# A GLU output stage in five passes over its tokens, with four token tiles' third quarter at the end

## The chip, the cores and the metric

The kernel runs on one core of a Trainium2 chip. The metric is the device time of one execution in microseconds (us), as a median over several executions; lower is better. The engines are named as in the profile: PE (matrix multiplies and transposes), DVE (vector operations), ACT (activations, copies and casts), POOL, and SP, which issues nearly all DMAs. Each engine runs its own instructions strictly in the order in which they were placed in its stream and waits for others by semaphores.

## The reference, cut to what matters

The model is a decoder trunk of two layers that runs on a prompt of 1024 tokens and on 64 sample tokens. Layer 0 mixes with a state-space model whose output goes through a gated linear unit (GLU), is normed, is added to the residual, and then goes through a convolutional feed-forward net (FFN):

```python
z = jax.nn.gelu(y).astype(u.dtype)
gl = z @ w_glu                                     # w_glu: 1024 x 2048
out = gl[..., :D_MODEL] * jax.nn.sigmoid(gl[..., D_MODEL:])
...
x = x + rmsnorm(a_out, p['a_post_g'][i])           # x1: goes to DRAM and on
f_out, buf = conv_ffn(rmsnorm(x, p['f_pre_g'][i]), ...)   # first step: h = x @ w_up
```

`rmsnorm(x, g)` is `x * rsqrt(mean(x*x) + eps) * g` over the 1024 channels of a token.

## The kernel before, in words

**Tiles.** Tokens lie in eight prompt tiles of 128 (numbers 0 to 7) and one sample tile of 64 (`NTT`, number 8). Multiplies are done in float32 split into a high and a low part, so each product is three matmuls (`mm3`, L800 to L802); the parts of the input are `xT_hi` and `xT_lo`, those of a weight `whi` and `wlo`.

**The GLU stage** (`glu`) runs four passes, one for each quarter `q` of the output channels (256 of them, with their 256 gates). In a pass, `tok_mm` does 24 matmuls of 128x512 for each prompt tile (16 for the sample tile) in the order `ORDER_U = [0, 3, 1, 4, 2, 5, 6, NTT, 7]`; then ACT takes the sigmoid of the gate half (L1022) and DVE multiplies (L1023) into columns `q*256...` of `ao[tt]`, an `acc` slot of 1024 columns that is held for the tile from the first pass to the last. A pass needs four units of weights (`load_w`): two DMAs of 256 KB into one of two `raw` buffers, a cast to `whi` on ACT (L783) and a subtraction to `wlo` on DVE (L784). `whi` and `wlo` rotate through 11 slots.

**The tails.** In the last pass, `tail.add` follows each tile's product. `tail_a` loads the residual row `xr` (L825), takes the sum of squares over 1024 columns on ACT (L815), multiplies by the post-norm gain over 1024 columns on DVE (L829), forms the reciprocal root in eight small DVE operations (`rstd_from`, L118 to L126), multiplies and adds the residual (L832) and stores the row to `x1d` (L833). `tail_n` does square, root and gain of the next norm (L842). Two tiles later (`lag`) `pop` transposes the tile on PE (L848) and splits it into `xT_hi` (ACT, L136) and `xT_lo` (DVE, L137). For the pairs of tiles (0,3), (1,4), (2,5), `Combos.pair` first forms four sums and differences of the two (L889 to L892, DVE), and transposes these, for the fast multiplication that follows.

**The FFN's first step** (`ffn_up(0)`) loads two blocks of `w_up`, forms their sums on DVE (L1076 to L1079, in the two `xr` slots) and begins with product p1 over tiles 0 to 2, first on channels 0 to 511 and then on the others; the next products need the combinations of all three pairs; the last ones need tiles 6, 7 and `NTT`.

**Order.** A scheduler sets the order of instructions on each engine when the kernel is built; tile pools (`acc` 14 slots, `gr` 5, `xr` 2) tell when a buffer is free again.

Of the kernel before, what the change touches and what calls it, by code (L numbers as in the profile page):

```python
# [20 lines left out]
P = 128  # L21
# [52 lines left out]
def trunk_kernel(ctx, tc, I, O):  # L74
# [33 lines left out]
    def flat(t, n=512):  # L108
        return t[:, 0:n]

    def rstd_from(pool, ss, n, parts, tag, n_mean=D, bufs=None):

        kw = {"bufs": bufs} if bufs else {}
        v = pool.tile([P, n], F32, tag=tag + "v", name=nm("rv"), **kw)
        s = pool.tile([P, n], F32, tag=tag + "s", name=nm("rs"), **kw)
        r = pool.tile([P, n], F32, tag=tag + "r", name=nm("rr"), **kw)
        p = slice(0, parts)
        V.tensor_scalar(v[p], ss, -0.5 / n_mean, -0.5 * EPS, op0=ALU.mult, op1=ALU.add)  # L118
        V.tensor_scalar(r[p].bitcast(I32), v[p].bitcast(I32), -0.5, RSQ_MAGIC, op0=ALU.mult, op1=ALU.add)
# [684 lines left out]
    def tokens(tt):  # L804
        return (tt * P, P) if tt < NTT else (SEQ, TS)
# [6 lines left out]
    def square_sum(y, n):  # L812
        junk = slot("junk", dtype=BF16)
        ss = slot("ss")
        A.activation(junk[0:n], y, AF.Square, accum_out=ss[0:n])  # L815
        return ss[0:n]

    def rms_rstd(t, n):
        return rstd_from(pools["ph"], square_sum(t, n), 1, n, "n1", bufs=4)

    def tail_a(y, tt, post, xsrc, xdst, last=False):

        t0, n = tokens(tt)
# [74 lines left out]
    class Tail:  # L898
# [6 lines left out]
        def add(self, y, tt, *a):  # L905
            tail_a(y, tt, *a)
# [86 lines left out]
    def glu(ws):  # L993

        zt = slot("acc")[0:TS, 0:D]
        zv = zt.rearrange("r (b g c) -> r b g c", g=8, c=16)
        for u in range(3):
            for j in range(min(3, 8 - 3 * u)):
                zs = zsd.rearrange("(b u) r w -> u r b w", u=3)[u, 32 * j : 32 * j + NB]
                nc.sync.dma_start(zv[:, :, 3 * u + j], zs.rearrange("s b (t c) -> (s t) b c", c=16))  # L1000
        post = row_bcast(I["a_post_g"][0])
        tail.gain = row_bcast(I["f_pre_g"][0])
        ao = {}
        for q in range(4):
            if q:
                ws = glu_units(q)
            qs_ = slice(q * 256, (q + 1) * 256)
            for tt in ORDER_U:
                n = tokens(tt)[1]
                if q == 0:  # L1010
                    ao[tt] = slot("acc")
                    if tt == ORDER_U[4]:
                        tail_b(zt, NTT)
                        xsx = sample_pair()
# [6 lines left out]
                sg = slot("gr")  # L1021
                A.activation(sg[0:n, 0:256], g[:, 256:512], AF.Sigmoid)  # L1022
                V.tensor_tensor(ao[tt][0:n, qs_], g[:, 0:256], sg[0:n, 0:256], ALU.mult)  # L1023
                if q == 3:
# [1006 lines left out]
```

## Time and profile before

| | |
|---|---|
| median of 3 executions | 2728.16 us (2722.85 to 2728.78) |
| the profiled execution, its own time | 2735.15 us |
| its span in the trace | 2733.4 us |
| PE busy | 2508.6 us, 92% of the span |
| DVE busy | 1958.1 us, 72% |
| ACT busy | 1261.3 us, 46% |
| POOL busy | 688.7 us, 25% |
| mean granted clock of PE | 0.972 |

The profile is one execution; the time of 2735.15 us is that execution's, and the 1.75 us beyond its span lie around it. A share of busy time is a mean over stages that differ, so the rows further below are taken from the stretch in which the GLU stage ends and the FFN begins (225 to 520 us). In a row, "idle before <- releaser" tells how long an engine stood still before an instruction and what ended that. PEclk 1.00 is the upper level of the matrix engine's clock, 2.4 GHz; values between 0.5 and 1.00 are means over a stretch with both levels.

### The profile page before, as it was taken

The page shows a single profiled execution, that of the slowest core. Times are in us where ns is not written, and L with a number is a line of the kernel's source. Part 1 is how long each engine was busy: PE and PEld are TensorE (multiplying, and loading weights), DVE is VectorE, ACT ScalarE, POOL GpSimd, SP SyncE. Part 2 cuts the span into 40 slices and gives each one's busy share as a digit, 9 for nine tenths or more (in the row PEclk, how much of TensorE's full clock was granted, in tenths as well). Part 3 has the DMA queues.
Part 4 walks back from the last instruction along what each step waited for, and adds up shares of the span by engine and source line. Part 5 has one row for each costly group of instructions (what it writes and reads, how often), then busy time and mean ns, then how long its engine had stood idle before and what let it go on. Part 6 is the DMA issues. An engine that isn't in the chain of part 4 may idle for free. (4 is left out here: it accounts for less than half of the span.)

```text
span 2733.4 us, 39285 instructions
## 1 busy us (share of the span) xinstructions
PE 2508.6 (92%) x14234; PEld 2203.3 (81%) x14234; DVE 1958.1 (72%) x3721; ACT 1261.3 (46%) x2477; POOL 688.7 (25%) x943
## 2 busy tenths in 40 slices
PE   3878997999999989999999899999699999998995
PEld 3767886999999967778776788877599999996774
DVE  7993349677777699884223688966877767779998
ACT  6762224444444454344322677853544444454332
POOL 3220000111332275401211222200011222237651
PEclk9999998999999999999999999999899999999998
DMA  5432322122222233344646433325222222233324
GB/s 143 106 93 76 92 65 92 61 73 74 77 79 75 91 110 90 113 138 174 204 154 206 107 87 83 92 85 171 85 73 72 73 72 73 72 108 102 103 82 146
DMA packets 257701, 278.61 MB, mean 102 GB/s; under 512 B 41772, under 2 KB 205924, under 8 KB 257508
## 3 DMA queue, kind: packets, MB, share of 16 engines
q1 hardware_dynamic: 253188, 263.85, 31.3%
q0 software_dynamic: 3232, 10.29, 1.7%
q8 instruction: 113, 1.85, 0.3%
q10 hardware_dynamic: 1088, 1.97, 0.2%
q14 instruction: 80, 0.66, 0.1%
HBM read 187.82 MB, written 68.58 MB: 94 GB/s over the span
## 5 line engine op out<-in xcount | busy, mean ns | idle before, releaser
L800 PE MATMUL mm<-xT_hi,whi 128*128 128x320 f32 (+1 forms) x1408 | 459.4, 328 | 6.1 <-ACT xT_hi L136 2.8
L801 PE MATMUL mm<-xT_lo,whi 128*128 128x320 f32 (+1 forms) x1408 | 456.3, 324 | 0.1
L802 PE MATMUL mm<-xT_hi,wlo 128*128 128x384 f32 (+1 forms) x1408 | 454.7, 324 | 0.0
L1162 POOL COPY cvo<-acc 128x2 f32<-128x2 f32 x88 | 157.4, 1788 | 675.6 <-ACT acc L1145 675.6
L137 DVE TENSOR_TENSOR wlo<-raw,whi 128x1024 fp32r<-128x1024 f32 x88 | 107.6, 1222 | 239.4 <-PE mm L801 233.3
L800 PEld LDWEIGHTS mm<-xT_hi,whi 128*128 128x128 f32 x1408 | 265.1, 189 | 15.1 <-DVE acc L1128 9.6
L801 PEld LDWEIGHTS mm<-xT_lo,whi 128*128 128x128 f32 x1408 | 266.1, 189 | 0.9 <-DVE xT_lo L137 0.9
L802 PEld LDWEIGHTS mm<-xT_hi,wlo 128*128 128x128 f32 x1408 | 265.5, 189 | 0.3
L1159 DVE SCALAR_TENSOR_TENSOR acc<-acc,cpar,acc 128x1104 f32<-128x1104 f32 x176 | 239.3, 1380 | 0.8 <-ACT acc L1157 0.5
L800 PE MATMUL mm<-whi,xT_hi 128*128 128x512 f32 x576 | 228.5, 401 | 4.0 <-ACT whi L783 4.0
L801 PE MATMUL mm<-wlo,xT_hi 128*128 128x512 f32 x576 | 229.1, 399 | 0.5 <-DVE wlo L784 0.5
L802 PE MATMUL mm<-whi,xT_lo 128*128 128x512 f32 x576 | 229.1, 399 | 0.0
L136 ACT CAST whi<-raw 128x1024 fp32r<-128x1024 f32 x88 | 92.6, 1052 | 282.3 <-PE mm L802 265.7
L1384 DVE TENSOR_TENSOR acc<-mm,acc 128x512 f32<-128x512 f32 x279 | 184.3, 680 | 11.1 <-PE mm L802 10.2
L800 PE MATMUL mm<-acc,whi 128*128 128x384 f32 x528 | 179.6, 341 | 4.9 <-DVE acc L1119 3.1
L801 PE MATMUL mm<-acc,whi 128*128 128x384 f32 x528 | 179.5, 340 | 0.0
L802 PE MATMUL mm<-acc,wlo 128*128 128x384 f32 x528 | 179.4, 340 | 0.0
L800 PEld LDWEIGHTS mm<-whi,xT_hi 128*128 128x128 f32 x576 | 108.7, 189 | 33.2 <-ACT whi L783 4.2
L801 PEld LDWEIGHTS mm<-wlo,xT_hi 128*128 128x128 f32 x576 | 108.8, 189 | 26.8 <-DVE wlo L784 0.9
L802 PEld LDWEIGHTS mm<-whi,xT_lo 128*128 128x128 f32 x576 | 108.8, 189 | 26.6 <-issue 0.8
L1157 ACT ACTIVATE acc<-acc,cpar 128x1104 f32<-128x1104 f32 x88 | 115.4, 1313 | 30.9 <-DVE acc L1128 20.2
L1846 DVE CUSTOM_DVE_ANT_0 S<-mm,tb 128x512 f32<-128x512 f32 (+3 forms) x192 | 101.2, 552 | 29.0 <-PE mm L1844 25.7
(561 smaller groups left out, 6238.6 us busy)
## 6 DMA issues: line engine op xcount, KB each, us to landing
raw<-in_w_up_dram SPq DMA_DIRECT2D x88, 512.0 KB
gd<-acc SPq DMA_DIRECT2D x44, 552.0 KB
raw<-in_w_down_dram SPq DMA_DIRECT2D x44, 512.0 KB
gr<-gd SPq DMA_DIRECT2D x80, 256.0 KB
raw<-in_glu_w_dram SPq DMA_DIRECT2D x32, 256.0 KB
acc<-in_cache_k_dram SPq DMA_DIRECT2D x16, 512.0 KB
acc<-in_cache_v_dram SPq DMA_DIRECT2D x16, 512.0 KB
xj<-in_x_prompt_dram SPq DMA_DIRECT2D x8, 512.0 KB
```

Of the source, the lines that this page charges most:

```text
L136: A.copy(hi_ap, ps_ap)
L137: V.tensor_tensor(lo_ap, ps_ap, hi_ap.bitcast(F32), ALU.subtract)
L800: PE.matmul(out, lh, rh, start=start, stop=False, **kw)
L801: PE.matmul(out, lh, rl, start=False, stop=False, **kw)
L802: PE.matmul(out, ll, rh, start=False, stop=stop, **kw)
L1157: A.activation(hc, hb[:, 2 : 2 + TG], AF.Identity, bias=cp[:, ft, 3:4], scale=cp[:, ft, 2:3])
L1159: V.scalar_tensor_tensor(hc, hb[:, tap : tap + TG], cp[:, ft, tap : tap + 1], hc, op0=ALU.mult, op1=ALU.add)
L1162: GP.tensor_copy(co[:, 0:2], hb[:, SEQ : SEQ + 2])
L1384: V.tensor_tensor(a, ps, a, ALU.add)
L1846: V.tensor_tensor_reduce(S_[j][:, k0 : k0 + w], ps[:, 0:w], H["tb"][:, b0 : b0 + w], 0.125, -3e38, ALU.add, ALU.max, mx[:, j, c : c + 1])
```

## The change

Five passes take the place of four, as (quarter, tiles, tiles whose tail follows):

- quarter 0, all tiles; quarter 1, all tiles;
- quarter 2, only `EARLY = [NTT, 0, 3, 1, 4]`;
- quarter 3, all tiles in the order `ORDER_O = [NTT, 0, 3, 1, 4, 2, 5, 6, 7]`; the tails of `EARLY` follow their products here;
- quarter 2 again, only `LATE = [2, 5, 6, 7]`, with their tails.

The weights of quarter 2 are therefore loaded, cast and subtracted twice. For a tile's quarters other than its last, the new `part` takes the sum of squares over 256 columns (ACT), adds it to a running sum (`pre`, DVE, L834) and multiplies by the post-norm gain (DVE, L838). `tail_a` then squares and multiplies only the last 256 columns, and `rstd_from` takes the running sum in. The four late tiles no longer hold an `acc` slot from the first pass on: their quarters 0, 1 and 3 are formed in the free half of a `gr` slot, stored to a DRAM tensor `aod` (12 stores of 128 KB), and come back in the last pass (8 loads, 512 and 256 columns) into an `acc` slot taken there. No matmul and no transpose is added or taken away.

```diff
+    EARLY, LATE = ORDER_O[:5], ORDER_O[5:]
...
+    def part(y, tt, post, cs):
+
+        n = tokens(tt)[1]
+        ss = square_sum(y, n)
+        if tt in sums:
+            p = sums[tt]
+            V.scalar_tensor_tensor(p, ss, -0.5 / D, p, op0=ALU.mult, op1=ALU.add)
+        else:
+            p = sums[tt] = pools["ph"].tile([P, 1], F32, tag=f"pre{tt}", name=nm("pre"), bufs=1)[0:n]
+            V.tensor_scalar(p, ss, -0.5 / D, -0.5 * EPS, op0=ALU.mult, op1=ALU.add)
+        V.tensor_tensor(y, y, post[0:n, cs], ALU.mult)
...
-        ss = square_sum(y, n)
-        for hs in halves:
+        ss = square_sum(y[:, rest], n)
+        for hs in halves if last else (rest,):
             V.tensor_tensor(y[:, hs], y[:, hs], post[0:n, hs], ALU.mult)
-        r = rstd_from(pools["ph"], ss, 1, n, "n1", bufs=4)
+        r = rstd_from(pools["ph"], ss, 1, n, "n1", bufs=4, pre=sums.pop(tt, None))
...
-        for q in range(4):
-            if q:
+        for q, tts, end in ((0, ORDER_U, ()), (1, ORDER_U, ()), (2, EARLY, ()), (3, ORDER_O, EARLY), (2, LATE, LATE)):
+            if q or end:
                 ws = glu_units(q)
...
+                if end is LATE:
+                    for cs in (slice(0, 512), slice(768, D)):
+                        nc.sync.dma_start(ao[tt][:, cs], aod[t0 : t0 + n, cs])
...
+                yq = ao[tt][0:n, qs_] if tt in ao else sg[:, 256:512]
+                V.tensor_tensor(yq, g[:, 0:256], sg[:, 0:256], ALU.mult)
+                if tt in end:
...
+                    tail.add(ao[tt][0:n, 0:D], tt, post, x_in, x_scr(x1d), rest=qs_)
+                else:
+                    part(yq, tt, post, qs_)
+                    if tt in LATE:
+                        nc.sync.dma_start(aod[t0 : t0 + n, qs_], yq)
+                        tail.norm()
+                        tail.pop()
```

In the changed kernel's order the lines have moved: L805 to L807 are the matmuls (before L800 to L802), L868 the transposes (L848), L141 the low-part evacuations (L137), L1049 the GLU product (L1023), L849, L852 and L862 the post-norm product, the residual and the gain (L829, L832, L842), L909 to L912 the pair's sums (L889 to L892), L783 the loads of GLU weights (L778), L1107 to L1110 the sums of `w_up` (L1076 to L1079).

**PE where the GLU stage ends.** Before, behind the last three GLU matmuls (`mm_3945`, the last prompt tile) stand eight groups of four transposes (the rest of tile 1, the five of the pair (1,4), two of tile 2; `gr` is a pair's sum or difference, `acc` a tile's normed row), and then the FFN's first product `mm_4103`:

```order
L800 MATMUL mm_3945<-whi_3314,xT_hi 128x512
L801 MATMUL mm_3945<-wlo_3315,xT_hi 128x512
L802 MATMUL mm_3945<-whi_3314,xT_lo 128x512
L848 MATMUL tr_3755<-ident,acc_2401 128x128 x4
L848 MATMUL tr_3832<-ident,gr_3824 128x128 x4
L848 MATMUL tr_3839<-ident,acc_2430 128x128 x4
L848 MATMUL tr_3846<-ident,gr_3825 128x128 x4
L848 MATMUL tr_3855<-ident,gr_3826 128x128 x4
L848 MATMUL tr_3864<-ident,gr_3827 128x128 x4
L848 MATMUL tr_3931<-ident,acc_2459 128x128 x4
L848 MATMUL tr_3938<-ident,acc_2459 128x128 x4
L800 MATMUL mm_4103<-xT_hi,whi_4081 128x384
```

Of the changed kernel, behind the last GLU matmuls (`mm_4138`, tile 7) stand two groups, of tile 2, and then the FFN's first product `mm_4261`:

```order
L806 MATMUL mm_4138<-wlo_3950,xT_hi 128x512
L807 MATMUL mm_4138<-whi_3949,xT_lo 128x512
L868 MATMUL tr_4200<-ident,acc_3955 128x128 x4
L868 MATMUL tr_4207<-ident,acc_3955 128x128 x4
L805 MATMUL mm_4261<-xT_hi,whi_4239 128x384
L806 MATMUL mm_4261<-xT_lo,whi_4239 128x384
L807 MATMUL mm_4261<-xT_hi,wlo_4240 128x384
L805 MATMUL mm_4261<-xT_hi,whi_4239 128x384
```

After the first 12 matmuls of that product come the transposes of the pair (2,5); `gr_4290` is that pair's first difference and `acc_4005` tile 5:

```order
L805 MATMUL mm_4261<-xT_hi,whi_4239 128x384
L806 MATMUL mm_4261<-xT_lo,whi_4239 128x384
L807 MATMUL mm_4261<-xT_hi,wlo_4240 128x384
L868 MATMUL tr_4298<-ident,gr_4290 128x128 x4
L868 MATMUL tr_4305<-ident,acc_4005 128x128 x4
L868 MATMUL tr_4312<-ident,gr_4291 128x128 x4
L805 MATMUL mm_4261<-xT_hi,whi_4239 128x384
L806 MATMUL mm_4261<-xT_lo,whi_4239 128x384
```

So six of the eight groups that stood between the last GLU matmul and the FFN's first one are now inside the GLU stage; the pair (2,5) stands behind the first 12 matmuls of the FFN's first product, as it did before.

**DVE where the GLU stage ends.** Before, around the last tile's GLU product (L1023, on `mm_3945`) stand the root's small operations of two other tiles, pair evacuations, and that tile's post-norm product over 1024 columns:

```order
L118 TENSOR_SCALAR rv_3919<-ss_3917 128x1
L1023 TENSOR_TENSOR acc_2588<-mm_3945,gr_3970 128x256
L137 TENSOR_TENSOR acc_3353<-tr_3855,acc_3349 128x2x128
L137 TENSOR_TENSOR acc_3353<-tr_3846,acc_3349 128x128
L119 TENSOR_SCALAR rr_3905<-rv_3903 64x1
L119 TENSOR_SCALAR rr_3921<-rv_3919 128x1
L122 SCALAR_TENSOR_TENSOR rs_3904<-rr_3905,rv_3903 64x1
L122 SCALAR_TENSOR_TENSOR rs_3920<-rr_3921,rv_3919 128x1
L126 SCALAR_TENSOR_TENSOR rr_3905<-rs_3904,rr_3905 64x1
L126 SCALAR_TENSOR_TENSOR rr_3921<-rs_3920,rr_3921 128x1
L829 TENSOR_TENSOR acc_2588<-acc_2588,acc_2339 128x1024
```

Of the changed kernel, from the last tile's GLU product (L1049, on `mm_4138`) on:

```order
L1049 TENSOR_TENSOR acc_4135<-mm_4138,gr_4163 128x256
L130 SCALAR_TENSOR_TENSOR rr_4109<-rs_4108,rr_4109 128x1
L130 SCALAR_TENSOR_TENSOR rr_4125<-rs_4124,rr_4125 128x1
L126 SCALAR_TENSOR_TENSOR rs_4108<-rr_4109,rv_4107 128x1
L141 TENSOR_TENSOR xT_lo<-tr_4200,xT_hi 128x4x128
L126 SCALAR_TENSOR_TENSOR rs_4124<-rr_4125,rv_4123 128x1
L130 SCALAR_TENSOR_TENSOR rr_4109<-rs_4108,rr_4109 128x1
L141 TENSOR_TENSOR xT_lo<-tr_4207,xT_hi 128x4x128
L849 TENSOR_TENSOR acc_4135<-acc_4135,acc_2340 128x256
L122 SCALAR_TENSOR_TENSOR rv_4172<-ss_4169,pre_2668 128x1
L130 SCALAR_TENSOR_TENSOR rr_4125<-rs_4124,rr_4125 128x1
L852 SCALAR_TENSOR_TENSOR acc_4070<-acc_4070,rr_4109,xr_4101 128x1024
```

The post-norm product is over 256 columns, and what stands behind the GLU product are the root of one more tile and two evacuations. Further on in the changed kernel's DVE order stands the pair's first difference (L909), which the PE order above waits for:

```order
L852 SCALAR_TENSOR_TENSOR acc_4135<-acc_4135,rr_4174,xr_4166 128x1024
L126 SCALAR_TENSOR_TENSOR rs_4189<-rr_4190,rv_4188 128x1
L1109 TENSOR_TENSOR xr_4234<-raw_4229,raw_4231 128x512
L1110 TENSOR_TENSOR xr_4234<-raw_4229,xr_4233 128x512
L130 SCALAR_TENSOR_TENSOR rr_4190<-rs_4189,rr_4190 128x1
L909 TENSOR_TENSOR gr_4290<-acc_4005,acc_3955 128x512
L910 TENSOR_TENSOR gr_4292<-acc_4005 128x512
```

Ahead of it stand the last tile's residual step (L852) and the sums of `w_up`.

**SP at the last change of weights.** Before, the loads of the last pass's four units stand in a row and `w_up` behind them:

```order
L778 DMA raw_3292<-in_glu_w_dram 128x2x256 x2
L778 DMA raw_3299<-in_glu_w_dram 128x2x256 x2
L778 DMA raw_3306<-in_glu_w_dram 128x2x256 x2
L778 DMA raw_3313<-in_glu_w_dram 128x2x256 x2
L1071 DMA raw_4071<-in_w_up_dram 128x8x128
L1071 DMA raw_4073<-in_w_up_dram 128x8x128
```

Of the changed kernel, the last unit's two loads (`raw_3948`, the fourth of the last pass) stand behind stores to `aod` (tiles 5 and 6, quarter 3), and the loads from `aod` behind the first block of `w_up`:

```order
L1057 DMA aod<-gr_3689 128x256
L1057 DMA aod<-gr_3787 128x256
L783 DMA raw_3948<-in_glu_w_dram 128x2x256
L1057 DMA aod<-gr_3835 128x256
L783 DMA raw_3948<-in_glu_w_dram 128x2x256
L1102 DMA raw_4229<-in_w_up_dram 128x8x128
L1036 DMA acc_3955<-aod 128x512
L1036 DMA acc_3955<-aod 128x256
L1036 DMA acc_4005<-aod 128x512
L1036 DMA acc_4005<-aod 128x256
```

SP has taken stores into its row that wait for DVE, and the weights' loads stand between them.

## Rows read from the trace of the kernel before

**Rows 1.** Busy time by stretch; columns: stretch, length, engines busy (instructions), PEclk, DMA share, GB/s.

```profile
225.00:389.00 164.00, 162.86 (x719) 130.45 (x720) 41.18 (x84) 32.98 (x55) 0.96 (x2) 0.98 0.26 73
305.00:345.00 40.00, 40.00 (x173) 32.23 (x173) 8.74 (x13) 7.59 (x13) 0.00 (x0) 1.00 0.16 53
389.00:431.00 42.00, 42.00 (x199) 34.13 (x197) 38.19 (x123) 19.88 (x41) 0.00 (x0) 1.00 0.37 126
431.00:451.00 20.00, 7.09 (x32) 5.21 (x32) 19.60 (x59) 10.14 (x23) 0.00 (x0) 0.60 0.27 93
451.00:456.00 5.00, 4.83 (x15) 3.78 (x13) 5.00 (x12) 2.02 (x4) 0.00 (x0) 0.53 0.24 52
431.00:500.00 69.00, 49.11 (x268) 44.31 (x268) 59.86 (x135) 34.52 (x62) 5.82 (x12) 0.83 0.24 76
500.00:520.00 20.00, 20.00 (x124) 19.82 (x123) 12.34 (x15) 9.01 (x13) 2.58 (x8) 1.00 0.18 61
```

**Rows 2.** Waits of PE in the GLU stage, 225 to 431 us (total, times, longest).

```profile
PE mm L800 <- ACT whi L783: 4.0, 1, 4.0
```

**Rows 3.** Waits of PE from the GLU stage's end on, 425 to 500 us.

```profile
PE tr L848 <- DVE rr L119: 4.3, 1, 4.3
```

**Rows 4.** PE in order of time (start, us, operation, count, [idle before <- releaser]).

```profile
429.68 0.60 PE L848 MATMUL tr<-ident,acc 128*128 128x128 f32 x4
430.03 0.48 PE L802 MATMUL mm<-whi,xT_lo 128*128 128x512 f32 x1
...
430.80 0.40 PE L802 MATMUL mm<-whi,xT_lo 128*128 128x512 f32 x1
...
447.02 1.09 PE L848 MATMUL tr<-ident,gr 128*128 128x128 f32 x4 [4.28 <-DVE rr L119]
...
451.34 0.69 PE L800 MATMUL mm<-xT_hi,whi 128*128 128x384 f32 x1
```

**Rows 5.** PE's groups by line and form, 431 to 500 us: count | busy, mean ns | idle.

```profile
L800 PE MATMUL mm<-xT_hi,whi 128*128 128x384 f32 x25 | 10.0, 399 | 0.0
...
L800 PE MATMUL mm<-xT_hi,whi 128*128 128x320 f32 x23 | 7.1, 314 | 2.1 <-ACT xT_hi L136 2.1
...
L848 PE MATMUL tr<-ident,acc 128*128 128x128 f32 x36 | 6.5, 325 | 4.4 <-DVE xT_lo L137 2.9 <-DVE acc L137 1.5
L848 PE MATMUL tr<-ident,gr 128*128 128x128 f32 x32 | 6.2, 337 | 10.0 <-DVE rr L119 4.3 <-DVE gr L889 2.4 <-DVE acc L137 1.9
L800 PE MATMUL mm<-acc,whi 128*128 128x384 f32 x16 | 5.9, 366 | 1.7 <-DVE acc L1122 1.7
```

**Rows 6.** DVE's groups by line and form, 389 to 480 us, same columns.

```profile
L829 DVE TENSOR_TENSOR acc<-acc,acc 128x1024 f32<-128x1024 f32 x8 | 9.8, 1225 | 1.8 <-ACT gr L815 1.7
L137 DVE TENSOR_TENSOR xT_lo<-tr,xT_hi 128x512 fp32r<-128x512 f32 x14 | 9.4, 681 | 0.7 <-ACT xT_hi L136 0.7
...
L137 DVE TENSOR_TENSOR wlo<-raw,whi 128x1024 fp32r<-128x1024 f32 x3 | 3.7, 1220 | 1.6 <-ACT whi L136 1.2 <-PE mm L801 0.4
...
L1023 DVE TENSOR_TENSOR acc<-mm,gr 128x256 f32<-128x256 f32 x7 | 2.9, 419 | 0.2
```

**Rows 7.** DVE in order of time, after the GLU stage's last matmul.

```profile
434.46 0.69 DVE L890 TENSOR_TENSOR gr<-acc 128x512 f32<-128x512 f32 x1
435.07 1.28 DVE L842 SCALAR_TENSOR_TENSOR acc<-acc,rr,acc 128x1024 f32<-128x1024 f32 x1
436.26 0.22 DVE L122 SCALAR_TENSOR_TENSOR rs<-rr,rv 128x1 f32<-128x1 f32 x1
436.39 0.15 DVE L118 TENSOR_SCALAR rv<-ss 128x1 f32<-128x1 f32 x1
...
445.94 0.41 DVE L1023 TENSOR_TENSOR acc<-mm,gr 128x256 f32<-128x256 f32 x1
```

**Rows 8.** ACT's cast of one unit of GLU weights, 225 to 480 us.

```profile
L783 ACT CAST whi<-raw 128x1024 fp32r<-128x1024 f32 x16 | 16.8, 1051 | 33.1 <-DMA raw<-in_glu_w_dram 27.2 <-PE tr L1053 4.2 <-PE mm L801 1.8
```

**Rows 9.** Longest wait of PE where layer 0's ffn_up ends, 960 to 1000 us.

```profile
PE mm L1373 <- DVE xT_lo L137: 5.4, 1, 5.4
```

More of the change, by code (lines that the diff above doesn't have):

```diff
@@ L109, in flat, with rstd_from @@
         return t[:, 0:n]
-    def rstd_from(pool, ss, n, parts, tag, n_mean=D, bufs=None):
+    def rstd_from(pool, ss, n, parts, tag, n_mean=D, bufs=None, pre=None):
         kw = {"bufs": bufs} if bufs else {}
@@ L117, in rstd_from @@
         p = slice(0, parts)
-        V.tensor_scalar(v[p], ss, -0.5 / n_mean, -0.5 * EPS, op0=ALU.mult, op1=ALU.add)
+        if pre is None:
+            V.tensor_scalar(v[p], ss, -0.5 / n_mean, -0.5 * EPS, op0=ALU.mult, op1=ALU.add)
+        else:
+            V.scalar_tensor_tensor(v[p], ss, -0.5 / n_mean, pre, op0=ALU.mult, op1=ALU.add)
         V.tensor_scalar(r[p].bitcast(I32), v[p].bitcast(I32), -0.5, RSQ_MAGIC, op0=ALU.mult, op1=ALU.add)
@@ L814, in square_sum @@
         ss = slot("ss")
-        A.activation(junk[0:n], y, AF.Square, accum_out=ss[0:n])
+        A.activation(junk[0:n, 0 : y.shape[1]], y, AF.Square, accum_out=ss[0:n])
         return ss[0:n]
@@ L819, in rms_rstd, with tail_a @@
         return rstd_from(pools["ph"], square_sum(t, n), 1, n, "n1", bufs=4)
-    def tail_a(y, tt, post, xsrc, xdst, last=False):
+    sums = {}
+    def part(y, tt, post, cs):
[8 more added lines that the diff above has]
+        V.tensor_tensor(y, y, post[0:n, cs], ALU.mult)
+    def tail_a(y, tt, post, xsrc, xdst, last=False, rest=slice(0, D)):
         t0, n = tokens(tt)
@@ L903, in __init__, with add @@
             self.n, self.q, self.combos, self.gain, self.lag = [], [], None, None, 2
-        def add(self, y, tt, *a):
-            tail_a(y, tt, *a)
+        def add(self, y, tt, *a, **kw):
+            tail_a(y, tt, *a, **kw)
             self.norm()
@@ L1003, in glu @@
         ao = {}
-        for q in range(4):
-            if q:
+        for q, tts, end in ((0, ORDER_U, ()), (1, ORDER_U, ()), (2, EARLY, ()), (3, ORDER_O, EARLY), (2, LATE, LATE)):
+            if q or end:
                 ws = glu_units(q)
             qs_ = slice(q * 256, (q + 1) * 256)
-            for tt in ORDER_U:
-                n = tokens(tt)[1]
-                if q == 0:
+            for tt in tts:
+                t0, n = tokens(tt)
+                if tt in EARLY and q == 0 or tt in LATE and end is LATE:
                     ao[tt] = slot("acc")
-                    if tt == ORDER_U[4]:
-                        tail_b(zt, NTT)
-                        xsx = sample_pair()
+                if end is LATE:
+                    for cs in (slice(0, 512), slice(768, D)):
+                        nc.sync.dma_start(ao[tt][:, cs], aod[t0 : t0 + n, cs])
+                if q == 0 and tt == ORDER_U[4]:
+                    tail_b(zt, NTT)
+                    xsx = sample_pair()
                 ps = tok_mm(tt, ws, None if n == P else xsx)
@@ L1020, in glu @@
                     g = ps
[L1021 to L1024, printed above, removed]
+                sg = slot("gr")[0:n]
+                A.activation(sg[:, 0:256], g[:, 256:512], AF.Sigmoid)
+                yq = ao[tt][0:n, qs_] if tt in ao else sg[:, 256:512]
+                V.tensor_tensor(yq, g[:, 0:256], sg[:, 0:256], ALU.mult)
+                if tt in end:
                     if tt == 0:
                         tail.combos = Combos()
-                    y = ao[tt][0:n, 0:D]
-                    tail.add(y, tt, post, x_in, x_scr(x1d))
+                    tail.add(ao[tt][0:n, 0:D], tt, post, x_in, x_scr(x1d), rest=qs_)
+                else:
+                    part(yq, tt, post, qs_)
[3 more added lines that the diff above has]
+                        tail.pop()
             if q == 0:
@@ L1968, in trunk_kernel @@
     gd = dtile("gd", [NF, P, TG])
+    aod = dtile("aod", [SEQ, D])
     x3d = dtile("x3d", [T, D])
```

## The prediction, made before the changed kernel ran

> **What bounds the kernel now.** Read first the busy time by stretch. From 225 to 389 us, while the first three GLU passes and the start of the fourth run, PE is busy for 162.86 of 164.00 us and DVE for 41.18 [rows 1]. PE is the bound there: its one longer wait is 4.0 us for the first weights [rows 2]. From 389 to 431 us PE is still full (42.00 of 42.00) but DVE is nearly so too, 38.19 [rows 1]: the tails run there. Then it turns over: from 431 to 451 us PE is busy for 7.09 of 20.00 us and DVE for 19.60 [rows 1].
>
> The order of time shows what happens at the turn. The last GLU matmul starts at 430.80 and the FFN's first one only at 451.34 [rows 4]; between them PE waits for DVE, longest 4.28 us for a small operation of a root [rows 3, 4]. That the cause is a backlog of DVE is told by one row: the GLU product of the last tile, whose matmuls ended at 431, starts on DVE at 445.94 [rows 7], 15 us late, and behind it that tile's whole tail is still to be done.
>
> What PE loses is wall time less its work at full rate. From 431 to 500 us it has 25 + 16 + 23 triples of matmuls, 192 in all [rows 5], and 124 of the same kinds took 20.00 us when nothing waited [rows 1], 0.161 us each: 30.9 us. The 36 + 32 transposes [rows 5] are 17 groups of four, and the sample tile adds two; a group takes 0.35 us up to the next start, and delays that matmul by 0.08 more (busy 0.48 against 0.40 [rows 4]): 19 x 0.43 = 8.2 us. So 69.0 - 39.1 = **29.9 us are lost**. Two or three of them are clock: from 451 to 456 us the granted clock is 0.53, mostly the lower level, 1.2 GHz, after PE had stood idle for much of 20 us [rows 1]. The 29.9 us are all that the change can win here.
>
> **The change part by part.** *PE's own work* is the same 36 tile passes and transposes: nought.
>
> *Post-norm in quarters.* A product over 1024 columns takes 1225 ns, one over 256 columns (taken as the GLU product's) 419 ns [rows 6]. Four quarters are 1.68 us, 0.45 us more for a tile, 4.1 us for nine; but only 0.42 of them is left in a tail, 0.8 us less for each of nine tails. With 27 small additions of some 0.13 us (a start to the next, 436.26 to 436.39 [rows 7]), 3.5 us, and four more subtractions of weights at 1.22 us, 4.9 us [rows 6], DVE has 12.5 us more to do in all. About 10 of them fall where DVE is busy for a quarter of the time [rows 1]; PE hides them. Without that cover they would cost 12.5 us.
>
> The Trainium skill speaks against this part: "VectorE: DVE Perf Modes", section "The TRN2 errata — SBUF-src ops pay a fixed extra latency per instruction", says that each instruction pays a fixed cost, so that one large tile pays once and many small ones each time, and advises 512 elements or more. The rows agree that there is such a cost, (419 - 1.05 x 256) = 150 ns at a slope of (1225 - 419) / 768 = 1.05 ns. By the rule alone the part is a loss of 4.1 us and the forecast would be 2718; by the rows it lies in idle time of DVE.
>
> *Five early tails in pass four, four late ones in pass five.* This carries the gain. I walked DVE's changed order, each operation priced from one start to the next: 0.13 for a small one, 0.61 for 512 columns, 1.19 for a residual or gain step (434.46 to 435.07 to 436.26 [rows 7]), 0.35 and 1.15 for products of 256 and 1024 columns (0.07 under their durations [rows 6], the overlap that the rows in time show). From the start of quarter 3 to the last tile's product it has 118 small operations (15.3 us), 13 residual and gain steps (15.5), 10 evacuations of tiles (5.5), 12 of combinations (4.0, by width), five weight subtractions (5.7), eight sums of pairs (4.9) and products of 256 columns (some 9): 60 us. PE has in that stretch 12 prompt tiles of 24 matmuls at 0.231 us (40.00 / 173 [rows 1]), 66.5 us, 3.7 for the sample tile and 13 groups of transposes, 5.6: 76 us. So DVE is **ahead when the GLU ends**, where it was 15 us behind. From product to product in the late pass DVE has 4.1 to 4.6 us against 5.5 of PE.
>
> *What is late next.* Count from the last GLU matmul's end. Sigmoid and product take 0.8 us. PE does tile 2's two groups and 12 matmuls of the FFN's first product, until about 4 us, and then waits for the pair (2,5). Between the last product and that pair's first difference DVE has 22 small operations (2.9), three residual and gain steps (3.6), two evacuations (1.2), one subtraction of 1024 columns (1.15), five operations of 512 (3.05) and a product of 256 (0.35): 12.2 us. So PE stands **from 4 to 13 us**. DVE then has 12.7 us up to tile 7's gain step: pair sums, evacuations of combinations, weights. PE feeds on these in bits; its last combinations come at about 26, with some 3 us of its work left ahead of tile 7's transposes, and from 29 on nothing waits. In those 29 us PE did 60 matmuls (9.7 us) and 11 groups (4.7): 14.4. It loses 14 to 15 us; with about 1 for the lower clock after the 9 us of idleness, **15 to 16**.
>
> *A fourth change of weights.* The three changes that there were cost PE nothing visible [rows 2]. At the last one the chain for the fourth unit is: a slot free 1.4 us into tile 7 of quarter 3, subtraction of the second unit 1.2, load (no row shows one apart; between nought and the 4.0 us of the one wait for weights [rows 2]; I take 3, nearer to that wait, as a load was behind it), cast 1.05 [rows 8], subtraction 1.2: about 9 us. PE asks for it after the rest of tile 7, three groups and 18 matmuls, at 11 to 12 us. Cost 0 to 1.5 us; I take 0.5. SP has stores to `aod` in front of that load; each waits for a product that DVE has done by then.
>
> *The way through DRAM.* Twelve stores and eight loads on SP, and a `gr` slot held until its store has landed. A round trip was not seen in the trace. It is bounded below by nought (rows needed only a tile later) and above by the same 4 us as a load, once: I take 0.5, for the first late tile.
>
> *The rest of layer 0.* The order in `ffn_up` and `ffn_down` is shuffled though the code is the same. The largest single wait there is 5.4 us where `ffn_up` ends [rows 9]; it can go or double: nought, give or take 5.
>
> **Sum.** 29.9 - 15.5 - 0.5 - 0.5 = 13.4, call it **14 us**. For the profiled execution that is 2735.15 - 14 = 2721; it was 7 us above the median of its kind, so from the median 2728.16 - 14 = **2714 us**. With 3 us either way for the walk and part of the 5 for the rest of layer 0, 9 to 19 us of gain, 2709 to 2719.
>
> **The rivals.**
>
> - *DVE is behind at the end after all* (the walk assumes that it is never held up; but it waits in order for ACT's squares and evacuations, for loads of `xr` and for slots that PE frees). If half of the old 15 us of backlog remains, the end costs 23 us in place of 15.5: gain 7, 2721. For: DVE's largest stretch between two products of pass four is 8.3 us by my walk, over PE's 5.5. Against: 60 against 76 in sum.
> - *The end runs better.* The pair's sums come while PE still has work, or the wait of 5.4 us [rows 9] falls away: gain 20, 2708. Little speaks for it, as the order fixes what stands ahead of L909.
> - *It does not do what it says*: PE starts the FFN earlier and gives the time back at the `ffn_up` hand-over (5.4 doubled and some lower clock), or tiles 2 and 5, now last, are what the FFN needs first. Gain 0, 2728.
> - *Slower: weights come late at the short passes.* `raw` has two buffers and SP's row is in order, so a store to `aod` that waits for DVE holds the next unit. If each of the last three changes of weights costs as much as DVE's longest stretch between products, 8.3 us, 25 us are lost: 2728 - 14 + 25 = 2739. It decides from 14 / 3 = 4.7 us a change on, that is with a chain 7 us longer than the 9 worked out. Against it: the margin of 2 us and no such wait at the old changes [rows 2].
>
> **How the numbers follow.** Forecast 0.55, behind after all 0.17, better 0.10, given back 0.10, slower 0.08. Faster by over 0.2% (5.5 us, about what a measurement of this kernel can tell from no change): 0.55 + 0.10 + three quarters of 0.17, 0.78. Within 0.2%: 0.04 + 0.10 = 0.14. Slower 0.08. The range from 2703 to 2727 takes in the better case (20 and 5 more) and half of the case that gives back; some 0.15 is left out.
>
> **What would show it.** In the changed profile the last tile's GLU product should start on DVE within 2 us of its last matmul (before 15); the FFN's first product within 3 us (before 20.5), and then one wait of about 9 us of a transpose for L909 or what stands ahead of it. DVE's busy time in the first three passes should rise by some 10 us with PE still full. I am wrong in the mechanism if PE waits for `whi` or `wlo` at a change of weights, if DVE's last product is 5 us late or more, or if the end of the GLU comes later than before by more than 2 us.

## The result, and the profile after

| | before | changed |
|---|---|---|
| median | 2726.56 us (4 runs, 2722.85 to 2728.78) | 2710.01 us (4 runs, 2706.40 to 2718.47) |
| ratio, 95% interval | | 0.9945 (0.9918 to 0.9972) |
| span of the profiled execution | 2733.4 us | 2716.7 us |
| DVE busy | 1958.1 us | 1971.2 us |

The change is worth 15 us by the ratio (0.0055 x 2727), 16.7 by the two spans. The busy time by stretch of the changed kernel (stretch, length, then PE, PEld, DVE, ACT, POOL busy with their instructions, PEclk, DMA share, GB/s) answers to [rows 1]:

```profile
225.00:389.00 164.00, 163.60 (x738) 131.28 (x739) 71.19 (x215) 54.01 (x126) 0.55 (x1) 0.99 0.35 104
...
389.00:431.00 42.00, 42.00 (x208) 34.49 (x207) 35.56 (x99) 19.81 (x48) 0.00 (x0) 1.00 0.51 163
431.00:451.00 20.00, 9.69 (x44) 7.86 (x43) 19.67 (x49) 9.22 (x16) 2.36 (x4) 0.73 0.33 106
...
431.00:500.00 69.00, 58.69 (x343) 56.49 (x342) 53.86 (x98) 32.37 (x52) 8.30 (x20) 0.90 0.23 71
```

PE is full up to 431 us as before, though DVE now does 71.19 us of work up to 389 us (before 41.18). Up to 355 us, where quarter 3 begins, DVE is busy for 45.51 us against 33.29 before: these 12 us are mainly the work by quarters (some 10 were predicted). The rest are early tiles' tails that have moved there. From 431 to 500 us PE is busy for 58.69 us where it was for 49.11.

PE in order of time (start, duration, line, count, [idle before <- releaser]) answers to [rows 4], DVE in order of time to [rows 7]:

```profile
431.87 0.39 PE L807 MATMUL mm<-whi,xT_lo 128*128 128x512 f32 x1
...
433.38 0.44 PE L805 MATMUL mm<-xT_hi,whi 128*128 128x384 f32 x1 [0.24 <-ACT xT_hi L140]
...
436.03 0.34 PE L807 MATMUL mm<-xT_hi,wlo 128*128 128x384 f32 x1
444.93 1.09 PE L868 MATMUL tr<-ident,gr 128*128 128x128 f32 x4 [8.55 <-DVE gr L909]
...
447.39 1.09 PE L868 MATMUL tr<-ident,gr 128*128 128x128 f32 x4 [0.52 <-DVE gr L911]
449.11 0.69 PE L805 MATMUL mm<-xT_hi,whi 128*128 128x384 f32 x1 [0.64 <-ACT acc L1144]
...
450.24 0.52 PE L805 MATMUL mm<-xT_hi,whi 128*128 128x384 f32 x1
...
453.12 0.94 PE L868 MATMUL tr<-ident,gr 128*128 128x128 f32 x4
...
454.25 0.34 PE L806 MATMUL mm<-xT_lo,whi 128*128 128x384 f32 x1
```

```profile
432.78 0.42 DVE L1049 TENSOR_TENSOR acc<-mm,gr 128x256 f32<-128x256 f32 x1 [0.33 <-ACT gr L1047]
...
444.09 0.69 DVE L909 TENSOR_TENSOR gr<-acc,acc 128x512 f32<-128x512 f32 x1
```

The last GLU matmul starts at 431.87, the last tile's product on DVE at 432.78, 0.9 us later (before 15.1). The FFN's first product starts at 433.38, 1.5 us after the last GLU matmul (before 20.5). PE then works to 436.4, waits 8.55 us for the pair's first difference (L909, done on DVE at 444.8), and after two short waits, the last of them ended at 449.11, nothing holds it. From 445 to 453 us it runs at the lower level of its clock (granted clock 0.50, 1.2 GHz):

```profile
445.00:453.00 8.00, 6.84 (x24) 6.07 (x25) 8.00 (x14) 3.17 (x6) 1.08 (x2) 0.50 0.46 133
```

The waits of PE from 225 to 450 us, longest first, hold that one and the first weights' (the latter answers to [rows 2]):

```profile
PE tr L868 <- DVE gr L909: 8.6, 1, 8.6
PE mm L805 <- ACT whi L788: 4.2, 1, 4.2
```

So the GLU's end is as the prediction drew it. Two things further on are not. First, `ffn_down`: from its first matmul (L1373 before, L1404 after) to the first one of the sample queries (L1671 before) the profiled executions take 304.8 and 296.0 us. PE's waits in that stretch, before and after:

```profile
PE mm L800 <- DVE acc L1384: 7.5, 5, 2.1
PE mm L1373 <- DVE xT_lo L137: 5.4, 1, 5.4
```

```profile
PE mm L1404 <- ACT xT_lo L140: 3.8, 1, 3.8
PE mm L805 <- DVE acc L1415: 2.5, 3, 1.7
PE mm L1404 <- DVE xT_lo L141: 1.9, 1, 1.9
```

Secondly, where attention begins the changed kernel, by then 23.5 us ahead of the trace before, loses 7 us. PE's waits there, from 1380 to 1530 us, before and after:

```profile
PE tr L1868 <- DVE S L1860: 8.0, 1, 8.0
PE mm L800 <- ACT qwh L1761: 4.5, 1, 4.5
```

```profile
PE mm L805 <- ACT qwh L1792: 15.1, 1, 15.1
PE tr L1899 <- DVE S L1891: 3.6, 1, 3.6
```

The wait for the first q weights (`qwh`) grew from 4.5 to 15.1 us, and the one behind it, for the first softmax, fell from 8.0 to 3.6. From the sample attention's last matmul (L1632) to the first softmax's reciprocal (L1858) it is 27.8 us before and 34.5 after.

### The profile page after: what moved, and what is told of

The parts are those of the page before. It is cut to its first block, busy times and chain, and to the rows that moved or that the text cites. A ratio compares the mean times of both kernels' runs of the same rounds, so it can differ in the third digit from the quotient of the medians.

```text
span 2716.7 us, 39533 instructions
## 1 busy us (share of the span) xinstructions
PE 2498.3 (92%) x14234; PEld 2201.4 (81%) x14234; DVE 1971.2 (73%) x3779; ACT 1269.5 (47%) x2535; POOL 632.1 (23%) x943
## 4 chain that ended last, share of the span: by engine, by line
PE 38%; DVE 10%; DMA 3%; ACT 3%; issue 2%; POOL 1%; SPq 0%; DVEq 0%; POOLq 0%; ACTq 0%
PE mm L805 10%; PE mm L807 10%; PE mm L806 10%; DVE S L1877 2%; DVE acc L1415 1%; ACT S L1881 1%; PE mm L1404 1%; PE mm L1905 1%; DMA gr<-gd 1%; DVE S L1891 1%; DVE xT_lo L141 1%; PE tr L868 1%; DVE qx L1820 1%; DMA raw<-in_w_down_dram 1%; PE tr L1614 1%
## 5 line engine op out<-in xcount | busy, mean ns | idle before, releaser
L805 PE MATMUL mm<-xT_hi,whi 128*128 128x384 f32 (+1 forms) x1408 | 457.6, 327 | 3.5 <-ACT acc L1144 1.2
L806 PE MATMUL mm<-xT_lo,whi 128*128 128x384 f32 (+1 forms) x1408 | 456.0, 324 | 0.4 <-DVE xT_lo L141 0.4
L807 PE MATMUL mm<-xT_hi,wlo 128*128 128x384 f32 (+1 forms) x1408 | 453.4, 324 | 0.0
L1193 POOL COPY cvo<-acc 128x2 f32<-128x2 f32 x88 | 103.0, 1171 | 761.2 <-ACT acc L1176 761.2
L805 PEld LDWEIGHTS mm<-xT_hi,whi 128*128 128x128 f32 x1408 | 264.8, 189 | 9.4 <-DVE acc L1159 4.8
L807 PEld LDWEIGHTS mm<-xT_hi,wlo 128*128 128x128 f32 x1408 | 265.2, 188 | 0.1
L805 PE MATMUL mm<-whi,xT_hi 128*128 128x512 f32 x576 | 230.0, 403 | 4.2 <-ACT whi L788 4.2
L807 PE MATMUL mm<-whi,xT_lo 128*128 128x512 f32 x576 | 228.9, 398 | 0.0
L141 DVE TENSOR_TENSOR wlo<-raw,whi 128x1024 fp32r<-128x1024 f32 x88 | 107.6, 1222 | 166.2 <-PE mm L806 162.4
L1415 DVE TENSOR_TENSOR acc<-mm,acc 128x512 f32<-128x512 f32 x279 | 184.2, 679 | 9.7 <-PE mm L807 9.0
L805 PE MATMUL mm<-acc,whi 128*128 128x384 f32 x528 | 178.9, 339 | 2.5 <-DVE acc L1150 2.5
L807 PE MATMUL mm<-acc,wlo 128*128 128x384 f32 x528 | 179.3, 340 | 0.0
L805 PEld LDWEIGHTS mm<-whi,xT_hi 128*128 128x128 f32 x576 | 109.2, 190 | 33.8 <-ACT whi L788 4.4
L807 PEld LDWEIGHTS mm<-whi,xT_lo 128*128 128x128 f32 x576 | 108.3, 188 | 26.3 <-issue 0.8
L1188 ACT ACTIVATE acc<-acc,cpar 128x1104 f32<-128x1104 f32 x88 | 113.9, 1311 | 19.5 <-DVE acc L1159 10.4
```

The lines of the kernel that those rows point to most:

```text
L141: V.tensor_tensor(lo_ap, ps_ap, hi_ap.bitcast(F32), ALU.subtract)
L805: PE.matmul(out, lh, rh, start=start, stop=False, **kw)
L806: PE.matmul(out, lh, rl, start=False, stop=False, **kw)
L807: PE.matmul(out, ll, rh, start=False, stop=stop, **kw)
L1188: A.activation(hc, hb[:, 2 : 2 + TG], AF.Identity, bias=cp[:, ft, 3:4], scale=cp[:, ft, 2:3])
L1193: GP.tensor_copy(co[:, 0:2], hb[:, SEQ : SEQ + 2])
```

## The experiments

All are compared with the kernel before on their own chip; times are medians, ratios have a 95% interval. "Lost at the end" is the 70 us that follow the last GLU matmul, less the work that PE started in them at its full rate (0.174 us for 384 columns, 0.146 for 320, 0.43 for a group of four transposes); a few records are missing from the traces, so it is good to some 0.6 us. Set against the kernel before, it agrees to 0.4 us with the time from the first pass's sample tile to the first transposes of `ffn_up` (238.5 us before, 224.2 changed). The columns behind the ratio are read from each kernel's own profiled execution. One such trace holds some chance: from the first softmax to the end, where none of the kernels was meant to differ, they take between 1203 and 1215 us.

| kernel | ratio to before | last product late by | lost at the end | ffn_down | wait for qwh | sample attention to softmax |
|---|---|---|---|---|---|---|
| before | 1 | 15.1 | 29.2 | 304.8 | 4.5 | 27.8 |
| changed | 0.9945 | 0.9 | 15.2 | 296.0 | 15.1 | 34.5 |
| e5 changed, again | 0.9953 (0.9936 to 0.9969) | 0.9 | 15.5 | 294.1 | 14.9 | 33.8 |
| e1 quarters alone | 0.9938 (0.9916 to 0.9959) | 8.3 | 21.0 | 292.7 | 4.5 | 27.5 |
| e10 the same | 0.9934 (0.9919 to 0.9948) | 8.3 | 20.4 | 295.0 | 4.5 | 27.1 |
| e2 split alone | 0.9971 (0.9959 to 0.9982) | 2.2 | 18.9 | 294.3 | 15.1 | 34.8 |
| e3 changed, values moved | 0.9931 (0.9904 to 0.9959) | 0.9 | 16.0 | 293.6 | 1.3 | 27.8 |
| e9 the same | 0.9918 (0.9903 to 0.9933) | 0.9 | 15.5 | 293.6 | 1.3 | 28.4 |
| e4 before, values moved | 1.0035 (1.0019 to 1.0051) | 15.1 | 29.5 | 300.2 | 15.7 | 35.1 |
| e6 e3 with lag 1 | 0.9969 (0.9955 to 0.9984) | 0.9 | 14.2 | 302.4 | 3.2 | 27.1 |
| e7 parts doubled | 0.9962 (0.9948 to 0.9976) | 0.8 | 14.9 | 293.4 | 15.1 | 34.5 |
| e8 before with lag 1 | 0.9999 (0.9985 to 1.0013) | 18.9 | 26.1 | 298.8 | 4.5 | 27.4 |
| e11 three late tiles | 0.9936 (0.9921 to 0.9950) | 2.0 | 16.2 | 294.9 | 1.3 | 30.7 |

**The two halves of the change apart.** e1 keeps the square sums and products by quarters and drops the split:

```diff
-    EARLY, LATE = ORDER_O[:5], ORDER_O[5:]
+    EARLY, LATE = ORDER_U, []
...
-        for q, tts, end in ((0, ORDER_U, ()), (1, ORDER_U, ()), (2, EARLY, ()), (3, ORDER_O, EARLY), (2, LATE, LATE)):
+        for q, tts, end in ((0, ORDER_U, ()), (1, ORDER_U, ()), (2, ORDER_U, ()), (3, ORDER_U, ORDER_U)):
```

> Four passes as before, all nine tails in the last one, no way through DRAM; only the square sums and post-norm products by quarters stay. Theory (what counts is how far DVE is behind when the GLU's matmuls end, and the split of the tiles does most of it): the nine tails lose 0.8 us each, 7.2 us, on DVE, so the last tile's product starts some 8 us after its matmul in place of 15, PE loses 22 to 24 us between 431 and 500 us in place of 29.9, and the time is 6 to 8 us under the kernel before. Rival (the quarters do all, the split nothing): the product starts within 2 us and 14 to 17 us are won. Second rival (only the split counts): nothing is won, the product stays 15 us late.

Measured: 2707.37 us against 2721.23. The last product on DVE (its matmuls' last one started at 427.7) and PE's waits from 425 to 500 us:

```profile
436.04 0.41 DVE L1049 TENSOR_TENSOR acc<-mm,gr 128x256 f32<-128x256 f32 x1
```

```profile
PE tr L868 <- DVE acc L862: 3.5, 1, 3.5
PE tr L868 <- DVE rr L123: 2.7, 1, 2.7
PE tr L868 <- DVE xT_lo L141: 2.2, 2, 1.2
```

At the GLU's end the theory held: 8.3 us late, 21.0 us lost, some 8 won. In the total it did not: 14 us, as much as the whole change. The other 6 to 8 do not come from the GLU; `ffn_down` is 7.5 us shorter than in e4 and 12.1 shorter than in the trace before, and nothing is given back at the q projection. e10 repeats it (2706.66 against 2723.64):

> Four passes with the square sums and post-norm products by quarters, once more in more rounds. By the traces it wins 8 us at the GLU's end and some 6 in ffn_down and gives nothing back at the q projection: 0.993 to 0.996 of the kernel before, level with the whole change.

It came out so: 8.3 us late, 20.4 lost, no more than 4.5 for `qwh`.

e2 keeps the split and drops the quarters:

```diff
-                    tail.add(ao[tt][0:n, 0:D], tt, post, x_in, x_scr(x1d), rest=qs_)
+                    tail.add(ao[tt][0:n, 0:D], tt, post, x_in, x_scr(x1d))
...
-                    part(yq, tt, post, qs_)
```

> Five passes with the late tiles' quarters through DRAM, but squares and post-norm product over 1024 columns in each tail as before. Theory: pass four still gives DVE 12 tiles of PE time for five tails, so DVE ends 2 to 4 us behind; behind the last product stand 15.3 us up to the pair's first difference in place of 12.1, so PE waits 11 to 13 us for it (8.6 in the changed kernel) and the end of the GLU costs 19 to 21 us: 9 to 11 us won at 500 us against the kernel before. Rival (the quarters do all): 0 to 3 us won at 500 us.

Measured: 2713.96 against 2721.23; the product 2.2 us late, 18.9 us lost, 10 won, as the theory had it. PE's longest waits from 425 us on, and a row of DVE:

```profile
PE tr L868 <- DVE gr L909: 7.1, 1, 7.1
PE tr L868 <- issue: 4.4, 1, 4.4
```

```profile
433.86 1.28 DVE L862 SCALAR_TENSOR_TENSOR acc<-acc,rr,acc 128x1024 f32<-128x1024 f32 x1
```

The row calls 4.4 us "issue", with no releaser. They end at 435.24, 0.1 us after the gain step of tile 2 on DVE (L862, until 435.14), and it is for this step that the program makes these transposes wait. So PE waits 11.5 us for DVE, the 11 to 13 of the theory, but in two parts and only 7.1 of it for the pair. The halves win 8 and 10 us at the GLU's end and 14 together: both shorten the same backlog.

**Where the q projection loses.** POOL's load of head 0's values (`v<-vd`) in the kernel before, then POOL and SP of the changed kernel in order of time:

```profile
1495.36 0.88 POOL L1741 DMA_DIRECT2D v<-vd  x1 [9.44 <-DVE rr L126]
```

```profile
1462.57 0.89 POOL L1788 DMA_DIRECT2D kr<-kd  x1
1482.52 0.88 POOL L1772 DMA_DIRECT2D v<-vd  x1 [19.06 <-DMA od<-acc]
1483.42 1.91 POOL L1791 TENSOR_TENSOR qraw<-qraw,bpg 128x1024 f32<-128x1024 f32 x1
```

```profile
1469.20 11.44 SPq L1676 DMA_DIRECT2D od<-acc  x16
```

SP issues the last 16 stores of the sample attention's output (`od<-acc`) one after the other, 11.44 us. POOL's load of head 0's values waits 19.06 us for a store from that buffer, and the multiply of the first q weights (`qraw`), whose data had been asked for at 1461.6, stands behind it. In the changed program, as it is built, that output lies in the buffer at byte 93696 of a partition, within the 4096 bytes from 91136 on that the values take; before, it lay at 102912. Both sizes and the program text there are unchanged, and so is the order on every engine from the sample attention's output to the end of the attention: the 14 buffers are handed out as they come free, and the new order frees them in another sequence. Of the traces, only those of the five runs in which the two share bytes (changed, e2, e4, e5, e7) have POOL's load wait for these stores, 19.1 to 20.6 us. e3 and e4 move the values to byte 99328, which parts them from the output in the changed kernel and puts them on it in the kernel before (what is laid out behind the values, the first heads' scores among it, moves by the same 8192 bytes):

```diff
             def values_in(h):
+                if h == 0:
+                    for _ in range(2):
+                        at([P, NTT, VD], "oh", 2)
                 v = heads[h]["v"] = at([P, NTT, VD], f"v{h % 2}")
```

> The changed kernel with one thing more: in the attention's pool two tiles are laid out ahead of the values of head 0, so that these lie at another address, where the sample attention's output buffer does not lie. Theory (the 10 to 12 us that layer 0 had gained beyond the GLU are lost where the q projection begins, since the load of head 0's values waits until all 32 stores from the sample attention's output buffer have landed, and the multiply of the first q weights stands behind that load on POOL): PE's wait for the first qwh falls from 15.1 to 5 us or less and the time is 6 to 11 us under the changed kernel. Rival (something else is late at the same place, such as the first head's softmax): the wait moves, and the time stays within 3 us of the changed kernel.

> The kernel before with the same two tiles laid out ahead of head 0's values; there this puts the values on the buffer of the sample attention's output, where they did not lie. Theory of the shared address: PE's wait for the first qwh rises from 4.5 to 14 us or more and the time rises by 4 to 10 us over the kernel before. Rival (the address does not matter, the wait in the changed kernel comes from its earlier arrival): the wait stays at 4 to 6 us and the time within 3 us.

Measured: e3 2704.29 us and e4 2731.88 us, against 2721.23. PE's waits from 1380 to 1530 us in e3, then in e4:

```profile
PE tr L1902 <- DVE S L1894: 11.7, 1, 11.7
PE mm L1908 <- ACT wt L1903: 1.4, 1, 1.4
PE mm L805 <- ACT qwh L1795: 1.3, 1, 1.3
```

```profile
PE mm L800 <- ACT qwh L1764: 15.7, 1, 15.7
PE tr L1871 <- DVE S L1863: 3.6, 1, 3.6
```

The wait for `qwh` follows the address both ways: 15.1 to 1.3, and 4.5 to 15.7. Part of it goes into the next wait, for the first softmax (3.6 to 11.7, and 8.0 to 3.6); what is left is 6.7 us in the changed kernel (34.5 to 27.8) and 7.3 in the one before. e4 is slower than before by 0.35%, 9.5 us. Two more runs were to give the size against the changed kernel:

> The changed kernel with head 0's values at the other address, once more beside the two others of this comparison and in more rounds. If the shared address costs what the traces show (6 to 7 us between the sample attention and the first softmax), it stands 5 to 8 us under the changed kernel, at 0.991 to 0.994 of the kernel before, and under the quarters alone by the 5 to 6 us that the split wins at the GLU's end. If the second wait, for the first softmax, takes most of it back, it is level with the quarters alone, at 0.993 to 0.996.

> The changed kernel once more, on the chip of the three runs that stand beside it, so that they can be set against it. It should again be 12 to 18 us under the kernel before: some 14 us won at the end of the GLU, some 8 in ffn_down, some 7 given back where the q projection begins.

e9: 2702.77 against 2723.64, 0.9918. e5: 2708.35 against 2722.90, 0.9953. By these two, moving the values is worth 0.35%, some 9 us; by e3 and the first result it is 0.14%, 4 us, with intervals that overlap. The traces' 6.7 us lie between. **e9 has the lowest ratio of all the kernels**, clear of the kernel before and of the changed one in e5; its lead over the quarters alone on its own chip (0.9934) is within the intervals. POOL in e9, where the load no longer waits for the stores:

```profile
1460.15 0.89 POOL L1791 DMA_DIRECT2D kr<-kd  x1
1466.00 0.88 POOL L1775 DMA_DIRECT2D v<-vd  x1 [4.96 <-PE mm L1663]
1466.90 1.91 POOL L1794 TENSOR_TENSOR qraw<-qraw,bpg 128x1024 f32<-128x1024 f32 x1
```

**Is the added vector work hidden?** e7 puts one more operation of 256 columns behind each of the 27 products of `part`:

```diff
         V.tensor_tensor(y, y, post[0:n, cs], ALU.mult)
+        V.tensor_tensor(y, y, y, ALU.max)
```

> The changed kernel with a second operation of 256 columns (a maximum of the row with itself, which changes nothing) behind each of the 27 post-norm products of the first quarters: 27 times some 0.35 us, 9.5 us more on DVE. Theory (the vector work that the change adds to the first passes lies in DVE's idle time): DVE is busy 8 to 10 us longer up to 431 us, PE as before, and the GLU ends within 1 us of where it ended. Rival (an instruction of few columns costs its fixed price on the path): 4 us or more later.

Measured: 2708.84 against 2722.90, 0.9962, beside 0.9953 for e5. Busy time from 225 to 389 us, and PE's longest wait after:

```profile
225.00:389.00 164.00, 163.48 (x732) 131.08 (x733) 79.51 (x232) 53.50 (x124) 0.63 (x2) 0.98 0.35 104
```

```profile
PE tr L869 <- DVE gr L910: 8.8, 1, 8.8
```

DVE has 8.3 us more (79.51 against 71.19), PE is as full, and 14.9 us are lost at the end, not more. The rule of the Trainium skill that the prediction weighed ("VectorE: DVE Perf Modes", "The TRN2 errata — SBUF-src ops pay a fixed extra latency per instruction") says that many small instructions pay a fixed cost each. The trace agrees: a post-norm product of 256 columns took 419 ns in the changed kernel, more than a quarter of the 1225 ns that one of 1024 took before. Here that cost fell in time that DVE had to spare.

**Can the remaining 8.6 us go?** e6 is e3 with the late tails transposed one tile earlier (`tail.lag` 1 in the last pass in place of 2; its expectation says "later" of the same edit):

```diff
                 ws = glu_units(q)
+            if end is LATE:
+                tail.lag = 1
...
         tail.norm()
+        tail.lag = 2
```

> The changed kernel with head 0's values at the other address, and with the late pass's tails transposed one tile later in place of two, so that the sums of the pair (2,5) stand 6.4 us of DVE's work behind the last product in place of 12.1. Theory (PE's 8.6 us of waiting at the GLU's end is that chain on DVE): the wait falls to 2 to 4 us, PE wins 4 to 6 us there, and the time is 10 to 13 us under the changed kernel. Rival (what stands in front of the pair now comes behind it, and PE waits for that): the wait for the pair falls, others come up, and less than 2 us are won at the end of the GLU.

Measured: 2713.55 against 2722.90, 0.9969, worse than without it. PE's waits from 425 to 500 us:

```profile
PE tr L868 <- DVE gr L909: 3.0, 1, 3.0
PE mm L805 <- DVE acc L1156: 2.8, 1, 2.8
PE mm L805 <- ACT xT_hi L140: 2.1, 2, 1.8
```

The wait for the pair fell to 3.0, but 2.8 for the next products' sums and 2.1 for an evacuation came up: the rival. Of 15.5 to 16 us lost at the end only 1.5 went. From the first transposes of `ffn_up` to `ffn_down` it took 446.0 us in place of 443.4, and `ffn_down` took 302.4 us, 9 more than in e3, so the run as a whole lost.

e8 makes the same edit in the kernel before (again one tile earlier):

> The kernel before with the last GLU pass's tails transposed one tile later in place of two, nothing else. It changes the order at the GLU's end and, with it, the scheduler's order in layer 0's FFN. Theory for the GLU's end (DVE's backlog decides, not where the transposes stand): within 3 us of the kernel before at 500 us. Theory for layer 0 (the old order of ffn_down was an unlucky one, and any other wins): ffn_down takes 294 us, 6 to 10 us less. Rival: it stays at 300 to 305 us, and what the changed kernel won there comes from the change.

Measured: 2722.11 against 2722.90. The GLU's end came out at the edge of what its theory allowed (26.1 us lost against 29.2), and the 3.1 us won there went again up to `ffn_down` (446.5 us from the first transposes of `ffn_up`, 443.5 before). `ffn_down` took 298.8 us, near the 300.2 of e4. But the order in which DVE, ACT and POOL work there is, instruction for instruction, that of the kernel before in both of them: the edit did not shuffle `ffn_down`, so that e8 says nothing on whether any other order wins.

e11 takes three late tiles (`ORDER_O[:6]` and `ORDER_O[6:]`):

> The changed kernel with three late tiles (5, 6, 7) in place of four: tile 2 gets its third quarter in the third pass, holds its buffer through, and makes no way through DRAM. The sample attention's output then lies in another buffer than head 0's values. Theory: DVE works the same sum, 12.9 us lie between the last product and the pair's difference (12.1 with four), so the end of the GLU costs 15 to 17 us as with four; PE's wait for the first qwh is 5 us or less, not 15, and the time is 5 to 8 us under the changed kernel. Rival (tile 5 as the first of the last pass delays the pair): PE waits 12 us or more for the pair, and nothing is won over four late tiles.

Measured: 2707.08 against 2723.64, 0.9936. PE's waits where attention begins:

```profile
PE mm L1875 <- DMA kl<-kl: 5.1, 2, 4.4
PE tr L1899 <- DVE S L1891: 4.5, 1, 4.5
PE mm L1874 <- DVE qx L1820: 2.0, 1, 2.0
PE mm L805 <- ACT qwh L1792: 1.3, 1, 1.3
```

The wait for `qwh` is gone here too, with the values at their old address, since the sequence of buffers is another one once more: the sample attention's output now lies at byte 70656. But that is where head 0's keys (`kh`, `kl`) are laid out, and DVE waits there for the same stores:

```profile
DVE kl L141 <- DMA od<-acc: 7.1, 1, 7.1
```

The 5.1 us of PE for a DMA of `kl` follow from it: the shared address has another victim. The GLU's end is as with four (16.2 us), with 10.4 us of waiting for the pair, and of the 5 to 8 us expected in the total it won 2 to 5 (0.9936 against 0.9945 and 0.9953, with intervals that overlap).

## Why the prediction was right, step by step

- **The loss before**: 29.9 us predicted, 29.2 by starts and rates.
- **DVE ahead at the end**: right. From the start of quarter 3 to the last GLU matmul (354.3 to 432.1 us) DVE is busy for 62.3 us of PE's 77.8, where 60 and 76 were predicted, and the last product is 0.9 us late (predicted under 2). e1, whose nine tails all fall in one pass, is 8.3 us late, and e2, whose tails are longer, 2.2: the lateness follows the work per pass.
- **What is late next**: right, and close. The pair's difference was predicted to be done 13 us after the last GLU matmul's end; it was at 444.8, 12.7 us after 432.1. PE waited 8.55 us of the 9. The last wait ends 17 us after the end (29 predicted): PE, at the lower clock from 444.9 to 453.1, came to the last combinations after they were there. For that the clock cost more than the 1 us allowed: 12 matmuls at 0.32 us in place of 0.174 and three groups of transposes at about 0.88 in place of 0.43, 3 us. The sum of both is what was predicted: 15.2 us lost against 15 to 16.
- **Changes of weights and the way through DRAM**: 0.5 us each was too much. PE loses nothing between the first GLU weights and the last GLU matmul; the slower rival did not come up, nor did its pattern.
- **Vector work by quarters**: hidden, as e7 shows.
- **The rest of layer 0**, "nought, give or take 5": missed. `ffn_down` takes 293 to 296 us in the changed kernel and in e1, e2, e3, e5, e7, e9, e10 and e11, and 299 to 305 in the kernel before, e4, e6 and e8. The traces show what parts the two kinds: in the second, POOL's order in `ffn_down` is that of the kernel before, and so is DVE's but for two places near the end in e6; in the first, both are close to that of the changed kernel. In the first kind PE's waits for `acc` of L1384 (L1415 after) sum to 1.5 to 4.1 us, in the second to 6.1 to 7.5. That is 5 to 9 us won that the sum did not have; the size is loose, since the trace before and that of e4, with one order there, already differ by 4.6. Which exchange in the order decides it stays open; e6 shows that a small edit in the GLU stage is enough to bring the old order back.
- **What the sum left out**: the q projection, 7 us lost. The prediction has no term behind layer 0's FFN, that is, it took what follows to cost the same. The order of the attention is the same, but an equal order can wait for other things when its buffers lie elsewhere. This is the rival "it gives the time back", in another place than the one named.

So the term that the forecast was made of, 14 us at the GLU's end, measured 14.3 (the lead of PE over the trace before grows from 2.4 us at the sample tile of the first pass, where the change has not acted yet, to 16.7 at the first transposes of `ffn_up`). That the total of 15 agrees as well is luck: two terms outside the sum, 5 to 9 us won and 7 lost, nearly cancel. The split and its way through DRAM, which win 6 us at the GLU's end over the quarters alone, are paid for by the shared address: as it stands, the changed kernel is not measurably faster than e1 or e10 (0.9945 and 0.9953 against 0.9938 and 0.9934).

## What to carry to other kernels

When the engine that feeds the matrix engine is behind at the end of a stage, price its work from product to product against the matrix engine's time; moving tails into an earlier pass pays once the sum per pass fits, and then the chain behind the last product sets the end. After a change of order, compare where the buffers of later stages lie, not only the order: a load can start waiting for another stage's stores only because its address is now shared. Check a forecast by stage, since a right total can hide two wrong terms.

## What the runs showed of the hardware that was not expected

- 16 stores from one buffer that SP issues in a row took 11.44 us, 0.7 us each. The load into memory that overlaps this buffer, which the program makes wait for them, started 1.9 us after SP had issued the last (1480.64 to 1482.52).
- After 8.55 us without work for PE (436.4 to 444.93) matmuls of 384 columns started every 0.32 us until 452.8 and every 0.174 us from 454.07 on; from 445 to 453 us the granted clock is 0.50, the lower level.
- 1.6 MB that went to DRAM in rows of 1 KB and came back in rows of 1 and 2 KB (`aod`, 12 stores of 128 KB, eight loads) cost PE nothing that its waits show.
